# Sine and cosine ahead of the float32 head in SyncE's queue: a rotary embedding kernel on one core

## Chip, cores and metric

One core of a Trainium2 chip runs the whole kernel. The metric is the device time of one execution in microseconds (us). Engines are named as in the profile: DVE is VectorE, ACT is ScalarE, POOL is GpSimd, SP is SyncE; the core has 16 DMA engines, which the transfers of all queues share. The clock granted to TensorE was 1.00; the kernel has no matrix multiplication.

## The reference

```python
# x: (8, 2048, 16, 64), cos and sin: (2048, 32), all float32
x1 = x[..., :32]
x2 = x[..., 32:]
out1 = x1 * cos - x2 * sin      # cos and sin broadcast over batch and heads
out2 = x1 * sin + x2 * cos
out = concatenate([out1, out2], axis=-1)
```

Each of the 8 batches is 8.39 MB in and 8.39 MB out. Nothing is reused between batches but the two tables of 256 KB.

## The kernel before, in words

**Tiles.** A batch is one tile `xt` of 128 partitions by 16 rows of the sequence (J = 16) by 16 heads by 64, in float16. Five such tiles exist (NBUF = 5), so batch b + 5 takes the place of batch b. Loads (L52) and stores (L60) go through GpSimd's queue (q0 of the profile, "software_dynamic"), which converts from and to float32 on the way. A transfer of a whole tile is one instruction on POOL and 8 data packets on each of the 16 DMA engines.

**The opening.** The first two rows of batch 0 (JA = 2) don't come through GpSimd. SyncE loads them as float32 into the tile `head` (L36, 1 MB), then the tables `sin_f` (L44) and `cos_f` (L45), 256 KB each, through its own queue (q1, "hardware_dynamic"). ScalarE casts head into the first two rows of batch 0's tile (L84), makes `sin_h` of `sin_f` in two instructions (L88, and L89 with the sign turned) and `cos_h` of `cos_f` (L90). The remaining 14 rows of batch 0 come through GpSimd's queue as its first transfer.

**A rotation** is three VectorE instructions on a tile, or on some of its rows: `v` = swapped halves times sine (L73), `xt` times cosine in place (L79), plus `v` (L81). The first two rows of batch 0 are rotated first, by themselves, and the first of them is stored at once (L100); then the other 14 rows, then whole batches.

**The close.** The last batch goes out in three parts: rows 0 to 8 (L130) and 9 to 13 (L132) through GpSimd's queue, and the last two rows by a cast into `head` (L140) and SyncE (L141), which waits until the part of L130 has landed.

**What sets the order.** The program is handed to a planner, which orders each engine's instructions by their place in the program and by costs it estimates, and puts in the waits. The kernel adds a few edges that order GpSimd's queue without a wait ("NoSync"): the first row's store after load 1, load 2 after it, the rest of batch 0's store after it, the last part after the gate. By the trace GpSimd issued loads 0 and 1; the first row; loads 2, 3, 4; the stores of batch 0's rest and batch 1; loads 5 and 6; stores 2 and 3; load 7; stores 4, 5 and 6; the two parts of batch 7. POOL issues in that order, so an instruction that waits holds all behind it: loads 5, 6 and 7 each wait until the store of the batch whose tile they take has landed.

Of the kernel before, what the change touches and what calls it, by code (L numbers as in the profile page):

```python
# [1 line left out]

# [4 lines left out]


@with_exitstack  # L10
def kernel(
    ctx: ExitStack,
    tc: tile.TileContext,
    x: bass.AP,
    cos: bass.AP,
    sin: bass.AP,
    out: bass.AP,
):
    nc = tc.nc
    f16 = mybir.dt.float16  # L20
    f32 = mybir.dt.float32

    B, S, H, D = x.shape
    Dh = D // 2
    P = nc.NUM_PARTITIONS
    J = S // P
    NBUF = 5

    const_pool = ctx.enter_context(tc.tile_pool(name="rope_const", bufs=1))
    io_pool = ctx.enter_context(tc.tile_pool(name="rope_io", bufs=NBUF))  # L30
    tmp_pool = ctx.enter_context(tc.tile_pool(name="rope_tmp", bufs=1))

    JA = 2
    head = const_pool.tile([P, JA, H, D], f32)
    x0 = x[0].rearrange("(p j) h d -> p j (h d)", j=J)
    nc.sync.dma_start(  # L36
        out=head.rearrange("p j h d -> p (j h d)"),
        in_=x0[:, 0:JA, :].rearrange("p j f -> p (j f)"),
    )
    sin_f = const_pool.tile([P, J, Dh], f32)  # L40
    cos_f = const_pool.tile([P, J, Dh], f32)
    cos_h = const_pool.tile([P, J, Dh], f16)
    sin_h = const_pool.tile([P, J, D], f16)
    nc.sync.dma_start(out=sin_f, in_=sin.rearrange("(p j) d -> p j d", j=J))  # L44
    nc.sync.dma_start(out=cos_f, in_=cos.rearrange("(p j) d -> p j d", j=J))  # L45

    loads = []

    def load(b):
        xt = io_pool.tile([P, J, H, D], f16)  # L50
        j0 = JA if b == 0 else 0
        dma = nc.gpsimd.dma_start(  # L52
            out=xt[:, j0:J, :, :].rearrange("p j h d -> p (j h d)"),
            in_=x[b].rearrange("(p j) h d -> p j (h d)", j=J)[:, j0:J, :].rearrange("p j f -> p (j f)"),
        )
        loads.append(dma)
        return xt

    def store(b, xt, j0=0):
        return nc.gpsimd.dma_start(  # L60
            out=out[b].rearrange("(p j) h d -> p j (h d)", j=J)[:, j0:J, :].rearrange("p j f -> p (j f)"),
            in_=xt[:, j0:J, :, :].rearrange("p j h d -> p (j h d)"),
        )

    def rotate(xt, j0, j1):
        v = tmp_pool.tile([P, J, H, D], f16)
        n = j1 - j0
        js = slice(j0, j1)
        shape = [P, n, H, 2, Dh]
        sin_b = sin_h[:, js, :].rearrange("p j (e d) -> p j e d", e=2).unsqueeze(2).to_broadcast(shape)  # L70
        cos_b = cos_h[:, js, :].unsqueeze(2).to_broadcast([P, n, 2 * H, Dh])
        xe = xt[:, js, :, :].rearrange("p j h (e d) -> p j h e d", e=2)
        nc.vector.tensor_mul(  # L73
            out=v[:, js, :, :].rearrange("p j h (e d) -> p j h e d", e=2),
            in0=xe[:, :, :, ::-1, :],
            in1=sin_b,
        )
        xw = xt[:, js, :, :].rearrange("p j h (e d) -> p j (h e) d", d=Dh)
        nc.vector.tensor_mul(out=xw, in0=xw, in1=cos_b)  # L79
        xa = xt[:, js, :, :].rearrange("p j h d -> p (j h d)")  # L80
        nc.vector.tensor_add(out=xa, in0=xa, in1=v[:, js, :, :].rearrange("p j h d -> p (j h d)"))  # L81

    tiles = [load(b) for b in range(2)]
    nc.scalar.copy(  # L84
        out=tiles[0][:, 0:JA, :, :].rearrange("p j h d -> p (j h d)"),
        in_=head.rearrange("p j h d -> p (j h d)"),
    )
    nc.scalar.copy(out=sin_h[:, :, Dh:D], in_=sin_f)  # L88
    nc.scalar.mul(out=sin_h[:, :, 0:Dh], in_=sin_f, mul=-1.0)  # L89
    nc.scalar.copy(out=cos_h, in_=cos_f)  # L90
    rotate(tiles[0], 0, JA)
    def part(b, j0, j1):
        return (
            out[b].rearrange("(p j) h d -> p j (h d)", j=J)[:, j0:j1, :].rearrange("p j f -> p (j f)"),
            tiles[b][:, j0:j1, :, :].rearrange("p j h d -> p (j h d)"),
        )

    def store_rows(b, j0, j1):
        dst, src = part(b, j0, j1)
        return nc.gpsimd.dma_start(out=dst, in_=src)  # L100

    first = store_rows(0, 0, 1)
    tc.add_manual_dep(
        first.ins,
        loads[1].ins.name,
        mybir.DependencyInfo(mybir.DependencyClass.NoSync, mybir.DependencyReason.DATA),
        reason="order of the ring",
    )
    tiles += [load(b) for b in range(2, NBUF)]
    tc.add_manual_dep(  # L110
        loads[2].ins,
        first.ins.name,
        mybir.DependencyInfo(mybir.DependencyClass.NoSync, mybir.DependencyReason.DATA),
        reason="order of the ring",
    )
    for b in range(B):
        rotate(tiles[b], JA if b == 0 else 0, J)
        if b < B - 1:
            st = store(b, tiles[b], 1 if b == 0 else 0)
            if b == 0:  # L120
                tc.add_manual_dep(
                    st.ins,
                    first.ins.name,
                    mybir.DependencyInfo(mybir.DependencyClass.NoSync, mybir.DependencyReason.DATA),
                    reason="order of the ring",
                )
        if b + NBUF < B:
            tiles.append(load(b + NBUF))
    dst, src = part(B - 1, 0, 9)
    gate = nc.gpsimd.dma_start(out=dst, in_=src)  # L130
    dst, src = part(B - 1, 9, J - JA)
    rest = nc.gpsimd.dma_start(out=dst, in_=src)  # L132
    tc.add_manual_dep(
        rest.ins,
        gate.ins.name,
        mybir.DependencyInfo(mybir.DependencyClass.NoSync, mybir.DependencyReason.DATA),
        reason="order of the ring",
    )
    dst, src = part(B - 1, J - JA, J)
    nc.scalar.copy(out=head.rearrange("p j h d -> p (j h d)"), in_=src)  # L140
    end = nc.sync.dma_start(out=dst, in_=head.rearrange("p j h d -> p (j h d)"))  # L141
    tc.add_manual_dep(
        end.ins,
        gate.ins.name,
        mybir.DependencyInfo(mybir.DependencyClass.Sync, mybir.DependencyReason.DATA),
        reason="the last rows go out behind this part",
    )


# [1 line left out]
_INS = ['x', 'cos', 'sin']  # L151
_OUTS = [((8, 2048, 16, 64), 'float32')]


# [23 lines left out]
```

## Time and profile before

| What | Value |
|---|---|
| Median of 3 runs | 317.05 us (316.58 to 317.15) |
| The profiled execution: its time, its span | 316.67 us, 314.9 us |
| DVE, POOL, ACT busy | 209.1, 9.9, 6.8 us |
| Head: issued, landed after | 0.74, 4.8 us |
| Sine: issued, landed after | 1.16, 13.4 us |
| Cosine: issued, landed after | 1.63, 31.9 us |
| First rotation instruction; first row's store issued | 15.79; 36.95 us |
| Rotation of batch 0's rest begins | 36.69 us |
| Last rotation: begins, ends | 236.73, 262.9 us |
| SyncE's last transfer: issued, landed after | 305.64, 8.4 us |

The span runs from the first to the last instruction of the profiled execution. The page of the profile gives busy time by engine, then the span in 40 slices (each digit is a busy share in tenths; in the DMA row the mean of the 16 engines), the DMA queues, the chain of work that ended last, and the groups of instructions by line with the idle time ahead of them. Further views of the same trace used below are the waits, the instructions in order of time (start, duration, engine, line, operation, and in brackets the idle time before it and what ended that), the chain in order of time, and the records of the DMA packets (queue, size, start, duration).

### The profile page before, as it was taken

Reading aid. Unit: us, or ns where it says so; the run is one execution under the profiler, and the core shown is the slowest. Engines: PE = TensorE matmul, PEld = TensorE weight load, DVE = VectorE, ACT = ScalarE, POOL = GpSimd, SP = SyncE. Lnnn points to the kernel's source line nnn. Section 1 sums busy time; section 2 is a strip of 40 time slices with the busy share of each in tenths; the row PEclk is TensorE's granted clock in tenths of the full one; section 3 lists DMA queues with packets and bytes.
Section 4 is the critical chain, followed back from the end, with each engine's and each line's share of the span. In section 5 each row is a group of like instructions: output and inputs, shape, how many; then the busy total and the mean of one; then the engine's idle time right before and its main releaser. Section 6 shows DMA issues by size and latency. Waiting matters only on the chain.

```text
span 314.9 us, 122 instructions
## 1 busy us (share of the span) xinstructions
DVE 209.1 (66%) x27; ACT 6.8 (2%) x6; POOL 9.9 (3%) x22
## 2 busy tenths in 40 slices
DVE  0010699999999999999999999995009993000000
ACT  4100000000000000000000000000000002000000
POOL 1000200000000000010000000200000001000000
DMA  9899999999999899999999999999999999999997
GB/s 280 184 262 206 200 266 200 200 262 204 200 200 325 375 492 407 400 350 250 200 200 237 362 400 400 491 441 266 200 316 416 400 400 524 408 400 400 433 443 323
DMA packets 3168, 101.71 MB, mean 323 GB/s; under 512 B 352, under 2 KB 352, under 8 KB 736
## 3 DMA queue, kind: packets, MB, share of 16 engines
q0 software_dynamic: 2592, 99.09, 98.1%
q1 hardware_dynamic: 576, 2.62, 2.2%
HBM read 67.63 MB, written 67.11 MB: 428 GB/s over the span
## 4 chain that ended last, share of the span: by engine, by line
DVE 25%; DMA 22%; issue 18%; another core or an unknown queue 17%; ACT 1%; POOL 1%; SPq 0%; POOLq 0%; DVEq 0%; ACTq 0%
DMA xt<-in_x_dram 12%; DMA cos_f<-in_cos_dram 10%; DVE xt L81 8%; DVE xt L79 8%; DVE v L73 8%; ACT head L140 1%; POOL out_dram L60 0%; POOL xt L52 0%; ACT cos_h L90 0%; SPq L44 0%; SPq L36 0%; POOLq L52 0%; DVEq L73 0%; ACTq L140 0%
## 5 line engine op out<-in xcount | busy, mean ns | idle before, releaser
L73 DVE TENSOR_TENSOR v<-xt,sin_h 128x16384 f16<-128x16384 f16 (+2 forms) x9 | 69.7, 7744 | 36.0 <-DMA xt<-in_x_dram 20.0
L79 DVE TENSOR_TENSOR xt<-xt,cos_h 128x16384 f16<-128x16384 f16 (+2 forms) x9 | 69.7, 7744 | 17.4 <-ACT cos_h L90 17.2
L81 DVE TENSOR_TENSOR xt<-xt,v 128x16384 f16<-128x16384 f16 (+2 forms) x9 | 69.7, 7745 | 0.3
L52 POOL DMA_DIRECT2D xt<-in_x_dram x8 | 4.4, 556 | 110.4 <-DMA out_dram<-xt 109.6
L140 ACT CAST head<-xt 128x2048 f32<-128x2048 f16 x1 | 1.9, 1897 | 228.8 <-DVE xt L81 228.8
L60 POOL DMA_DIRECT2D out_dram<-xt x7 | 3.7, 535 | 63.6 <-DVE xt L81 63.6
L84 ACT CAST xt<-head 128x2048 f16<-128x2048 f32 x1 | 1.9, 1897 | 3.5 <-DMA head<-in_x_dram 3.5
L130 POOL DMA_DIRECT2D out_dram<-xt x1 | 0.5, 531 | 45.6 <-DVE xt L81 45.6
L100 POOL DMA_DIRECT2D out_dram<-xt x1 | 0.5, 536 | 34.5 <-DVE xt L81 34.5
L84 ACT ACT_TABLE_LOAD x1 | 1.3, 1283 | 0.7 <-PEq L162 0.7
L90 ACT CAST cos_h<-cos_f 128x512 f16<-128x512 f32 x1 | 0.6, 617 | 17.8 <-DMA cos_f<-in_cos_dram 17.8
L88 ACT CAST sin_h<-sin_f 128x512 f16<-128x512 f32 x1 | 0.6, 617 | 7.2 <-DMA sin_f<-in_sin_dram 7.2
L89 ACT ACTIVATE sin_h<-sin_f 128x512 f16<-128x512 f32 x1 | 0.6, 624 | 0.0
L132 POOL DMA_DIRECT2D out_dram<-xt x1 | 0.5, 531 | 0.0
L162 POOL MEMSET const-float32-0.0<- 128x1 f32 x1 | 0.1, 98 | 0.2 <-issue 0.2
L162 POOL MEMSET const-bfloat16-1.0<- 128x1 bf16 x1 | 0.1, 101 | 0.0
L162 POOL MEMSET const-float32-1.0<- 128x1 f32 x1 | 0.1, 98 | 0.0
L162 POOL MEMSET const-uint8-127<- 128x1 uint8 x1 | 0.1, 98 | 0.0
## 6 DMA issues: line engine op xcount, KB each, us to landing
xt<-in_x_dram POOLq DMA_DIRECT2D x7, 4096.0 KB, 38.3
out_dram<-xt POOLq DMA_DIRECT2D x1, 7680.0 KB, 60.9
out_dram<-xt POOLq DMA_DIRECT2D x1, 4608.0 KB, 42.4
xt<-in_x_dram POOLq DMA_DIRECT2D x1, 3584.0 KB, 22.3
out_dram<-xt POOLq DMA_DIRECT2D x1, 2560.0 KB, 47.9
head<-in_x_dram SPq DMA_DIRECT2D x1, 1024.0 KB, 4.8
out_dram<-head SPq DMA_DIRECT2D x1, 1024.0 KB, 8.4
out_dram<-xt POOLq DMA_DIRECT2D x1, 512.0 KB, 7.8
```

The costliest lines, as they stand in the source:

```text
L52: dma = nc.gpsimd.dma_start(out=xt[:, j0:J, :, :].rearrange("p j h d -> p (j h d)"), in_=x[b].rearrange("(p j) h d -> p j (h d)", j=J)[:, ...
L60: return nc.gpsimd.dma_start(out=out[b].rearrange("(p j) h d -> p j (h d)", j=J)[:, j0:J, :].rearrange("p j f -> p (j f)"), in_=xt[:, j0:J ...
L73: nc.vector.tensor_mul(out=v[:, js, :, :].rearrange("p j h (e d) -> p j h e d", e=2), in0=xe[:, :, :, ::-1, :], in1=sin_b,)
L79: nc.vector.tensor_mul(out=xw, in0=xw, in1=cos_b)
L81: nc.vector.tensor_add(out=xa, in0=xa, in1=v[:, js, :, :].rearrange("p j h d -> p (j h d)"))
L84: nc.scalar.copy(out=tiles[0][:, 0:JA, :, :].rearrange("p j h d -> p (j h d)"), in_=head.rearrange("p j h d -> p (j h d)"),)
L88: nc.scalar.copy(out=sin_h[:, :, Dh:D], in_=sin_f)
L89: nc.scalar.mul(out=sin_h[:, :, 0:Dh], in_=sin_f, mul=-1.0)
L90: nc.scalar.copy(out=cos_h, in_=cos_f)
L100: return nc.gpsimd.dma_start(out=dst, in_=src)
L130: gate = nc.gpsimd.dma_start(out=dst, in_=src)
L140: nc.scalar.copy(out=head.rearrange("p j h d -> p (j h d)"), in_=src)
```

## The change

SyncE's three opening DMAs are issued in the order sine, cosine, head instead of head, sine, cosine. Besides, the program is written in another form: a table `plan` lists the loads (L), rotations (R) and stores (S) with batch and rows, a loop runs it, and every transfer of GpSimd's queue has a NoSync edge to the one before it, where before a few had. The cast of head into batch 0's tile now stands in the program ahead of that tile's load by GpSimd; it stood behind the loads of batches 0 and 1. The sizes of the transfers, the tiles and their number, the arithmetic and the close are the same. The kind "L4" occurs in no row of the plan.

```diff
     head = const_pool.tile([P, JA, H, D], f32)
-    x0 = x[0].rearrange("(p j) h d -> p j (h d)", j=J)
-    nc.sync.dma_start(
-        out=head.rearrange("p j h d -> p (j h d)"),
-        in_=x0[:, 0:JA, :].rearrange("p j f -> p (j f)"),
-    )
...
     nc.sync.dma_start(out=sin_f, in_=sin.rearrange("(p j) d -> p j d", j=J))
     nc.sync.dma_start(out=cos_f, in_=cos.rearrange("(p j) d -> p j d", j=J))
+    x0 = x[0].rearrange("(p j) h d -> p j (h d)", j=J)
+    nc.sync.dma_start(
+        out=head.rearrange("p j h d -> p (j h d)"),
+        in_=x0[:, 0:JA, :].rearrange("p j f -> p (j f)"),
+    )
...
+    plan = (
+        ("L", 0, 2, 16), ("L", 1, 0, 16), ("R", 0, 0, 2), ("S", 0, 0, 1),
+        ("L", 2, 0, 16), ("L", 3, 0, 16), ("L", 4, 0, 16),
+        ("R", 0, 2, 16), ("S", 0, 1, 16), ("R", 1, 0, 16), ("S", 1, 0, 16),
+        ("L", 5, 0, 16), ("L", 6, 0, 16),
+        ("R", 2, 0, 16), ("S", 2, 0, 16), ("R", 3, 0, 16), ("S", 3, 0, 16),
+        ("L", 7, 0, 16),
+        ("R", 4, 0, 16), ("S", 4, 0, 16), ("R", 5, 0, 16), ("S", 5, 0, 16),
+        ("R", 6, 0, 16), ("S", 6, 0, 16), ("R", 7, 0, 16),
+    )
...
+    def ring(out, in_, **kw):
+        nonlocal last
+        dma = nc.gpsimd.dma_start(out=out, in_=in_, **kw)
+        if last is not None:
+            behind(dma, last, mybir.DependencyClass.NoSync)
+        last = dma
+        return dma
...
-    tiles = [load(b) for b in range(2)]
-    nc.scalar.copy(
-        out=tiles[0][:, 0:JA, :, :].rearrange("p j h d -> p (j h d)"),
-        in_=head.rearrange("p j h d -> p (j h d)"),
-    )
+    flat = head.rearrange("p j h d -> p (j h d)")
+    tiles[0] = io_pool.tile([P, J, H, D], f16, name="xt")
+    nc.scalar.copy(out=held(0, 0, JA), in_=flat)
     nc.scalar.copy(out=sin_h[:, :, Dh:D], in_=sin_f)
     nc.scalar.mul(out=sin_h[:, :, 0:Dh], in_=sin_f, mul=-1.0)
     nc.scalar.copy(out=cos_h, in_=cos_f)
...
+    for what, b, j0, j1 in plan:
+        if what == "L":
+            if b not in tiles:
+                tiles[b] = io_pool.tile([P, J, H, D], f16, name="xt")
+            ring(held(b, j0, j1), rows(x, b, j0, j1))
...
+        elif what == "S":
+            ring(rows(out, b, j0, j1), held(b, j0, j1))
+        else:
+            rotate(b, j0, j1)
```

## The prediction, as put on record

> **What bounds the kernel now.** I read the busy line by engine first, then the DMA lines of the page, then the waits, then the chain, and last the stretch around the change in order of time.
>
> ```profile
> span 314.9 us, 122 instructions
> ...
> DVE 209.1 (66%) x27; ACT 6.8 (2%) x6; POOL 9.9 (3%) x22
> ...
> DMA  9899999999999899999999999999999999999997
> ...
> q0 software_dynamic: 2592, 99.09, 98.1%
> q1 hardware_dynamic: 576, 2.62, 2.2%
> HBM read 67.63 MB, written 67.11 MB: 428 GB/s over the span
> ```
>
> No compute engine is near its span, but the sixteen DMA engines are busy in every slice: q0 (GpSimd's queue) 98.1% and q1 (SyncE's) 2.2% make 100%. Busy could still mean slow, so I check the pace with the waits of GpSimd's queue.
>
> ```profile
> 120.75 8.69 DVE L79 TENSOR_TENSOR xt<-xt,cos_h 128x16384 f16<-128x16384 f16 x1
> 121.38 0.53 POOL L52 DMA_DIRECT2D xt<-in_x_dram x1 [34.74 <-DMA out_dram<-xt]
> ...
> 140.66 0.53 POOL L52 DMA_DIRECT2D xt<-in_x_dram x1 [18.75 <-DMA out_dram<-xt]
> ...
> 198.37 0.53 POOL L52 DMA_DIRECT2D xt<-in_x_dram x1 [56.12 <-DMA out_dram<-xt]
> ...
> 236.73 8.69 DVE L73 TENSOR_TENSOR v<-xt,sin_h 128x16384 f16<-128x16384 f16 x1 [20.02 <-DMA xt<-in_x_dram]
> ```
>
> Each of these starts as a transfer lands: the rest of batch 0's store, batch 1's store, batch 2's store (behind the loads of 5 and 6), and the load of batch 7 (behind batch 3's store). Between them lie 1, 3 and 2 whole batches of 8.39 MB: 140.66 - 121.38 = 19.28, (198.37 - 140.66) / 3 = 19.24, (236.73 - 198.37) / 2 = 19.18 us. That is one steady 435 GB/s. The whole traffic at it, (67.63 + 67.11) MB / 435 GB/s, is 309.7 us of a 314.9 us span. So the queue is never empty, and the order and volume of its transfers set the end. The last DVE instruction ends at 262.9 us, 52 us ahead of it.
>
> The chain of waits tells another story at the start, and it is the change's story:
>
> ```profile
> 1.63 31.86 DMA cos_f<-in_cos_dram
> 33.49 0.02 issue
> 33.52 0.63 ACT cos_h L90
> 34.14 0.02 issue
> 34.17 1.24 DVE xt L79
> ```
>
> Cosine, 256 KB, takes 31.86 us and holds VectorE back. The trace's packet records say why (worked out per queue and size; times in us):
>
> ```
> queue   bytes  what            packets  start of first..last  one takes
> SyncE    8192  head            128       1.73 ..  4.86        0.309 (each engine's first 0.37 to 1.04)
> SyncE    2048  sine, cosine    256       4.72 .. 30.62        0.084 alone, 0.096 beside GpSimd's
> GpSimd  28672  batch 0 load    128       5.12 .. 20.99        2.129
> GpSimd  32768  batch loads 1-7 896      22.75 .. 233.91       2.431
> ```
>
> Each engine gets 8 data packets of every transfer and one small one for the semaphore. Up to 5.12 us it serves SyncE's alone; from 5.12 to 5.62, engine by engine, GpSimd's begin, and then one SyncE packet passes per GpSimd packet. Sine lands at 14.6, cosine at 33.5: nine turns of 2.1 to 2.4 us apart.
>
> **The change part by part.** *The plan of the GpSimd queue.* Its rows are, one by one, the order in which the trace shows GpSimd issuing: loads 0 and 1, one row of batch 0, loads 2 to 4, stores 0 and 1, loads 5 and 6, stores 2 and 3, load 7, stores 4 to 6, two parts of store 7. Same transfers, same instructions (22 on POOL), nothing added: 0 us. No added edge between two of them makes an engine wait for another.
>
> *SyncE's order.* SyncE issues at 0.74, 1.16 and 1.63 now and will again, with sine, cosine, head in the slots. Sine's first packet comes at about 1.73 (head's now does). Sine and cosine together take 16 x 0.084 = 1.34 us per engine; the cold first packets cost head now 4.72 - 1.73 - 8 x 0.309 = 0.5 us, which I take over. So head starts at 1.73 + 0.5 + 1.34 = 3.6 and by 5.4, when GpSimd's packets come, 1.8 / 0.309, some 5 to 6 of its 8 packets are through. Three or four are left with the semaphore's, each behind 2.13 us: head lands near 5.4 + 4 x 2.4 = 15, instead of 5.5. Bounds: 8, if only one is left; 5.6 + 9 x 2.44 = 27.6, if none has passed.
>
> *The path behind it.* ScalarE's cast of head takes 1.90, the two casts of sine (starts 14.61 and 15.13) 1.14 if they stay behind it, then VectorE's three instructions at 1.24: the first row of batch 0 is ready near 15 + 1.9 + 1.1 + 3.7 = 22 instead of 36.7 (34.3 by the late bound). The rest of batch 0 can start when its load has landed, at 1.25 + 22.3 = 23.6, instead of 36.69: VectorE is **13 us earlier**. The store of batch 0's rest is issued near 47 instead of 59.92, that of batch 1 near 73 instead of 86.11.
>
> *Where the 13 us go.* The stores join a queue that is full: loads 2 to 4 stand ahead of them. The rest of batch 0's store still lands at 120.8, so load 5 still waits for its buffer until 121.4: POOL's wait there grows from 34.74 to about 48. Rotations 2, 3 and 4 follow at 26.2 each (3 x 8.73) and end near 151.5; rotation 5 then waits for load 5, rotation 6 ends near 212, and rotation 7 waits for load 7, which lands at 236.7 as before. VectorE's 20.02 us there become about 25. Nothing after 236.7 moves. What is late next is the queue itself. Gain on the path: 0.
>
> *What is left is the work of the DMA engines.* The bytes are the same. In the window before GpSimd's packets there is enough from SyncE either way: sine, cosine and head last until 1.73 + 0.5 + 1.34 + 2.47 = 6.0, past 5.62, so no engine idles. Some twelve sine and cosine packets now served at 0.096 will be served at 0.084: -0.15. The cold start is not seen for 2048-byte packets: at best its 0.5 us vanishes (-0.65 in all); at worst each of the two later transfers pays another 0.5 (+1.0). I take about 0, since the cold cost is that of the first packet on an engine, and there is one in either order.
>
> The records price the small packets: 2048 bytes in 0.084 us are 24.4 GB/s per engine, head's 8192 in 0.309 are 26.5, and one SyncE packet passes per GpSimd packet. [...]
>
> **Sum.** The profiled execution took 316.67: the span of 314.9 and 1.77 around it. 316.67 + 0 = 316.7, with -0.65 to +1.0 as bounds. It lies 0.38 below the median of the runs, 317.05, so for the median I say **317.0**. About 0.2% (0.6 us) is what a measurement of this kernel can tell from no change.
>
> **Rivals.** *The early start reaches the end.* If the loads and stores could follow the rotations, 13 us would come off: 304. For it: the chain starts with cosine. Against it: 435 GB/s without a gap, and 20 us of waiting ahead of rotation 7. 2%.
>
> *A quicker start of the engines.* The cold cost nearly vanishes with small packets: 317.05 - 0.7 = 316.3. For it: it is the only slack in the stream. [...] 6%.
>
> *A slower start.* Cosine and head each pay their own cold start: 317.05 + 1.0 = 318.0. For it: three small starts in a row; against: sine's first packets behind head took at most 0.148. 5%.
>
> *Batch 0's load waits for ScalarE (slower).* In the new text the cast of head into batch 0's tile stands ahead of that tile's load. If the dependency were kept by tile and not by rows, POOL's first DMA would wait for it, and with it everything in POOL's queue. Head would then land alone at 6.5, the cast end at 8.4, the load be issued at 8.5 and, as now (5.12 - 1.25 = 3.9 later), move its first packet at 12.4. The engines would stand idle from 6.0: +6.4, **323.4**. It costs as soon as the load is issued after 6.0 - 3.9 = 2.1. Against it: now the load stands first, and the cast starts at 5.54, eighteen us before that load lands, into the same tile. 5%.
>
> *The change doesn't do what it says:* three loads with no dependency could still be ordered head first by the planner. Then 317.05. 3%.
>
> Head that comes very late is no rival of its own: POOL runs dry only if the first row's store is issued after load 1 has landed (23.6 + 8 x 2.43 = 43.0), and the late bound gives 34.3.
>
> **How the numbers follow.** The forecast has 79% (own range 316.5 to 317.6) and the planner's rival 3%: 82% within 0.2%. Faster: 6 + 2 = 8%. Slower: 5 + 5 = 10%. The range, 316.2 to 318.2, takes in the bounds of the cold start on the median and leaves out the 2% and the 5% far off.
>
> **What would show it.** Right: sine and cosine landed before 6 us, head near 15; batch 0's rest rotating near 24; the load of batch 5 still issued near 121.4, that of batch 7 near 198.4; a longer wait ahead of rotation 7; DMA slices all at 9. Wrong: a POOL wait ahead of batch 0's load, a low digit in the first DMA slice, a pace other than 19.2 us per batch, or a load of batch 7 that lands at another time than 236.7, with the difference in it.

## The result, and the profile after

The changed kernel takes 318.22 us in the median of 22 runs (316.39 to 319.39), the kernel before 316.94 (316.58 to 317.42, 22 runs): a ratio of 1.0034, 95% interval 1.0020 to 1.0049. It is slower by a third of a per cent, and its runs lie 3.0 us apart where those of before lie 0.8: nine of the 22 take 317.4 us or less, as before, the others up to 319.39. The forecast of no change was wrong; 318.22 lies just above the upper end of its range (318.2), and so near to it by chance, since the mechanism is one that none of its cases has.

The page of the changed kernel, the same lines as before:

```profile
span 317.6 us, 121 instructions
...
DVE 209.1 (66%) x27; ACT 6.7 (2%) x6; POOL 9.9 (3%) x22
...
DMA  8999999999999899999999999999999999999995
...
q0 software_dynamic: 2592, 99.09, 97.5%
q1 hardware_dynamic: 576, 2.62, 2.2%
HBM read 67.63 MB, written 67.11 MB: 424 GB/s over the span
```

The first slice of the DMA row is an 8 where a 9 stood, q0's share fell from 98.1% to 97.5%, and the span grew by 2.7. The profiled execution took 319.38 us, nearly the longest of the 22, so it shows the full loss; no trace of a shorter one exists. The bytes, packets and POOL instructions are the same. The instructions in order of time show where the 2.7 us came in:

```profile
0.74 0.38 SPq L39 DMA_DIRECT2D sin_f<-in_sin_dram  x1
1.17 0.43 SPq L40 DMA_DIRECT2D cos_f<-in_cos_dram  x1
...
1.64 0.42 SPq L42 DMA_DIRECT2D head<-in_x_dram  x1
3.61 0.62 ACT L123 CAST sin_h<-sin_f 128x512 f16<-128x512 f32 x1 [1.59 <-DMA sin_f<-in_sin_dram]
...
27.88 1.90 ACT L122 CAST xt<-head 128x2048 f16<-128x2048 f32 x1 [22.61 <-DMA head<-in_x_dram]
...
33.58 7.63 DVE L110 TENSOR_TENSOR v<-xt,sin_h 128x14336 f16<-128x14336 f16 x1
...
124.02 0.53 POOL L95 DMA_DIRECT2D xt<-in_x_dram  x1 [40.48 <-DMA out_dram<-xt]
...
143.32 0.53 POOL L95 DMA_DIRECT2D xt<-in_x_dram  x1 [18.76 <-DMA out_dram<-xt]
...
162.12 8.69 DVE L110 TENSOR_TENSOR v<-xt,sin_h 128x16384 f16<-128x16384 f16 x1 [0.87 <-DMA xt<-in_x_dram]
...
201.00 0.53 POOL L95 DMA_DIRECT2D xt<-in_x_dram  x1 [56.10 <-DMA out_dram<-xt]
...
239.39 8.69 DVE L110 TENSOR_TENSOR v<-xt,sin_h 128x16384 f16<-128x16384 f16 x1 [24.94 <-DMA xt<-in_x_dram]
```

The four events that were at 121.38, 140.66, 198.37 and 236.73 are at 124.02, 143.32, 201.00 and 239.39: later by 2.64, 2.66, 2.63 and 2.66. The pace between them is the old one, (201.00 - 143.32) / 3 = 19.23 us per batch. So nothing was lost between 124 and 239 us, and all of it before. VectorE meanwhile began the rest of batch 0 at 33.58 in place of 36.69 and waits 24.94 in place of 20.02 ahead of the last rotation: its lead is waited away, as the prediction has it.

The packet and semaphore records of the two traces show the loss itself. The 16 DMA engines post their semaphore steps one by one as their share of a transfer is done (352 landings for 22 transfers, 16 each); "first" and "last" are the earliest and the latest engine (us, worked out from the records). The records carry no engine's number: what is said here and below of single engines is worked out from the starts, ends and landings.

```
                                   before            after
SyncE packets per engine ahead
  of GpSimd's first                13 to 18          18 (sine, cosine)
GpSimd's first packets start       5.12 .. 5.62      3.35 .. about 5.7
engines at work, of 16, in
  3.5-4.0  4.0-4.5  4.5-5.0        16   16   16      11.5  11.8  12.6
  5.0-5.5  5.5-6.0  6.0-6.5        16   16   16      14.4  15.4  15.5
head's first packet                1.73              5.6
landing of       load 0            23.02 .. 23.55    23.39 .. 26.45
  first, last    rest of store 0   120.27 .. 120.79  121.03 .. 123.44
                 load 7            236.14 .. 236.64  236.90 .. 239.29
                 SyncE's last      313.52 .. 314.04  314.27 .. 316.74
```

Sine and cosine are through the engines by 3.4 to 3.8, and then more than a quarter of the engines (4.5 of 16) stand still, the last of them for some 2 us. Twelve engines have their first GpSimd packet by 4.09, four between 4.84 and 5.66. Every transfer is cut into 16 equal shares (each engine gets 8 data packets of it and one small one), and the engines that started some 2 us behind did not catch up: the distance between the first and the last engine is 3.1 us at load 0 and still 2.4 to 2.5 at the end of the kernel, where twelve engines post between 314.27 and 314.70 and four between 315.72 and 316.74.

Standing still is not all of it. On average an engine ended 1.2 us later (the mean of the 16 last steps is 313.71 before, 314.93 after). Of this, idle time after 3.5 us makes 0.5 ((4.5 + 4.2 + 3.4 + 1.6 + 0.6 + 0.5) x 0.5 / 16). Most of the rest is packets that took longer: GpSimd's first two on an engine took 2.33 and 2.42 us in the mean, where both took 2.13 before. Why they did is not shown. The time is that of the last engine, 2.7 us later.

### The profile page after: what moved, and what is told of

It is laid out like the page before. It is cut to its first block, busy times and chain, and to the rows that moved or that the text cites. A ratio compares the mean times of both kernels' runs of the same rounds, so it can differ in the third digit from the quotient of the medians.

```text
span 317.6 us, 121 instructions
## 1 busy us (share of the span) xinstructions
DVE 209.1 (66%) x27; ACT 6.7 (2%) x6; POOL 9.9 (3%) x22
## 3 DMA queue, kind: packets, MB, share of 16 engines
q0 software_dynamic: 2592, 99.09, 97.5%
## 4 chain that ended last, share of the span: by engine, by line
DVE 44%; DMA 20%; issue 18%; ACT 1%; POOL 0%; SPq 0%; DVEq 0%; ACTq 0%; POOLq 0%
DVE v L110 16%; DVE xt L118 14%; DVE xt L116 14%; DMA xt<-in_x_dram 12%; DMA head<-in_x_dram 8%; ACT xt L122 1%; ACT head L140 1%; POOL out_dram L95 0%; SPq L40 0%; SPq L39 0%; DVEq L110 0%; ACTq L140 0%; POOLq L95 0%
```

## The experiments

The leading theory was the hole: in the new order the DMA engines run out of work between SyncE's and GpSimd's packets, unequally, and the latest engine sets the end. The rivals: the new form of the program costs the time; tables in front cost it by themselves; head comes late, by its size, its place, or for another reason; GpSimd's start is uneven by itself. Kernels of one group ran on one chip beside the kernel before; ratios are to it, with 95% intervals, and differ slightly from the quotient of the medians. In the code below, (head) stands for head's load and `...` for what is left out of a line.

### The form alone, and the order alone

`e1_form_only` is the new form with SyncE's old order; `e2_order_only` is the old form with SyncE's new order.

```diff
 # e1, against the changed kernel
+    (head)
     nc.sync.dma_start(out=sin_f, ...)
     nc.sync.dma_start(out=cos_f, ...)
-    (head)
 # e2, against the kernel before: the same lines the other way round
```

> The plan's form with SyncE's old order (head, sine, cosine). Gap theory (after sine and cosine the DMA engines have nothing to do for up to 2 us, unequally, and the latest one stays behind to the end): head is 64 KB per engine and covers that time, so GpSimd's first packets start within 0.6 us of each other, a landing's 16 semaphore steps stay within 0.6 us, and the time is that of before, 316.9 (ratio 0.999 to 1.001). Form theory (the cast ahead of the load in the program, or the edges, cost the time): 318.2, as the change.

> The old form with SyncE's order sine, cosine, head. Gap theory: 318.2 in the median, runs scattered from 316.4 to 319.4 as the latest engine's start falls, landings spread over 2 us or more. Form theory: 316.9, landings within 0.6 us.

Measured: e1 317.17 us, 0.9995 (0.9986 to 1.0004); e2 319.36 us (316.86 to 326.07), 1.0048 (1.0029 to 1.0068). The form is free, and the order alone is the whole effect. In the profiled execution of e1 (317.7 us, its longest) GpSimd's first packets start within 0.7 us of each other, but the landings of load 0 are 1.2 us apart and later ones 1.3, where 0.6 was expected: three of the first packets took 2.57 to 2.74 us and not 2.13. In that of e2 (319.39 us) they start from 3.46 to 5.75 and the landings stay 2.65 us apart to the end. One of e2's twelve executions took 326.07; the ratio leaves it out, no trace of it exists, and it stays unexplained.

### Two of the three in front

`e3_sin_head_cos` puts head second; `e4_tables_from_act` and `e8_head_from_act` use ScalarE's queue beside SyncE's.

```diff
 # e3, against the changed kernel, as e4 and e8
     nc.sync.dma_start(out=sin_f, ...)
-    nc.sync.dma_start(out=cos_f, ...)
     (head)
+    nc.sync.dma_start(out=cos_f, ...)
 # e4
-    nc.sync.dma_start(out=sin_f, ...)
-    nc.sync.dma_start(out=cos_f, ...)
+    nc.scalar.dma_start(out=sin_f, ...)
+    nc.scalar.dma_start(out=cos_f, ...)
 # e8
-    nc.sync.dma_start(out=head..., ...)
+    nc.scalar.dma_start(out=head..., ...)
```

> The plan's form with SyncE's order sine, head, cosine. Gap theory: sine's 16 KB and head's 64 KB per engine follow each other without a hole until about 1.73 + 0.5 + 0.67 + 2.47 = 5.4, so GpSimd's packets are covered and the time is 316.9, landings within 0.6 us; head lands near 5.8 and cosine, now the third, near 25. Rival (head is late because of its size or of the order, not because it stands third): head's first packet comes near 5.6 again, the hole opens already at 2.7 and the time is 318.2 or more.

> The plan's form, head issued by SyncE and both tables at the same time by ScalarE's queue. Gap theory: three transfers share the engines from 1.7 to about 6.0 without a hole, the time is 316.9 and landings stay within 0.6 us, although all three land before 8 and VectorE's rotation of batch 0's rest starts near 24 instead of 36.7. A theory by which the early rotation is worth something would have 304 to 316; one by which any early small transfer in front costs a cold start would have 318.

> The change with head issued by ScalarE's queue at the same time as the tables by SyncE's: tables in front as in the change, but the engines are fed until about 6.0. Gap theory: no hole, landings within 1 us, 316.4 to 317, although VectorE starts the rest of batch 0 near 24, 10 us ahead of the change. Rival (tables in front cost time by themselves): 318 to 319.5.

Measured: e3 316.62 us, 0.9981 (0.9972 to 0.9989); e4 316.78 us, 0.9982 (0.9973 to 0.9990); e8 316.82 us, 0.9987 (0.9978 to 0.9995). In all three the loss is gone, and 0.1 to 0.2% more. GpSimd's first packets start at 5.2 to 5.8, nearly all engines are at work from 2.5 us on and all from 3.0, and the landings at the end are 0.98, 0.35 and 0.60 us apart. So in e3 and e8 (0.9981, 0.9987) a small table in front cost nothing, with head's 8192-byte packets ahead of GpSimd's first as well. One expectation missed: cosine did not land early in e4 and e8. As the second of its queue it came behind GpSimd's first packets and landed at 26.13 and 23.99, so the rest of batch 0 began at 29.33 and 27.18, not at 24.

### No head, a short head, a small third transfer

`e5_no_head` drops head: all 16 rows of batch 0 come through GpSimd. `e7_short_head` has the old order with one row in head. `e6_third_small` puts a fourth, useless transfer of 98 KB between cosine and head.

```diff
 # e5, against the changed kernel
-    nc.sync.dma_start(out=head..., in_=x0[:, 0:JA, :]...)
-    nc.scalar.copy(out=held(0, 0, JA), in_=flat)
-        ("L", 0, 2, 16),
+        ("L", 0, 0, 16),
 # e6, against the changed kernel
+    again = const_pool.tile([P, 6, Dh], f32)
...
     nc.sync.dma_start(out=cos_f, ...)
+    nc.sync.dma_start(out=again, in_=sin.rearrange("(p j) d -> p j d", j=J)[:, 0:6, :])
 # e7, against e1: head[:, 0:1] and row 0 alone; the plan loads and rotates rows 1 to 15
-        ("L", 0, 2, 16),  ("R", 0, 0, 2),  ("R", 0, 2, 16),
+        ("L", 0, 1, 16),  ("R", 0, 0, 1),  ("R", 0, 1, 16),
```

> SyncE loads the two tables alone; all 16 rows of batch 0 come through GpSimd's queue, the same bytes in all. Gap theory (the hole is GpSimd's own uneven start once SyncE's packets are gone): its first packets again start anywhere from 3.4 to 5.9, landings spread over 2 us or more, the time is 318 to 319.5. Rival (head's late packets hold up some engines): without head the first packets start within 0.6 us of each other and the time is 316.5 to 317.

> The change with a small third transfer (six rows of sine again, 768 bytes per partition, into a tile that nobody reads) between cosine and head; head is the fourth. It adds 98 KB, 0.2 us of the engines. If the third place is what is late, the small transfer's first packet comes only near 5.6, behind GpSimd's first, and the hole stays: 318 to 319.5. If head was late for its size, the small transfer follows cosine by 3.7 without a hole of its own, and head's packets come near 5.6 behind it.

> The plan's form, SyncE's old order, but head has one row in place of two (512 KB; the other 15 rows of batch 0 come through GpSimd, the same bytes in all). Gap theory: SyncE's first two transfers last until 1.73 + 0.5 + 8 x 0.16 + 0.67 = 4.2 in place of 5.4, so about half the hole opens: landings spread over 1 to 2 us, 317.5 to 318.5. Rival (only which transfer stands first or last counts, not how long the engines are fed): 316.9 to 317.2, as with two rows.

Measured: e5 318.61 us (316.46 to 319.39), 1.0032 (1.0013 to 1.0051): the loss and the scatter of the change without any head at all. Fifteen engines get their first GpSimd packet at 3.42 to 3.83, one at 5.67, and that one keeps the landings 3.0 us apart. Head's late packets are not the cause.

e7 317.03 us (316.99 to 317.59), 0.9994 (0.9985 to 1.0002): my estimate missed. Half the cover cost nothing: SyncE's first two transfers end at 4.5 to 5.4, GpSimd's first packets start at 4.16 to 5.08, no engine stands still until 6.5. Here the hole did not grow in step with the time for which SyncE feeds the engines. All of head and sine, 18 packets on each engine, and none of cosine went ahead of GpSimd's first. It also shows that 5.12 us, which the prediction took for the time when GpSimd's packets come, is only when the lot of SyncE's packets ahead of them is done ("lot" here: the packets of SyncE that an engine runs ahead of GpSimd's first).

e6 327.39 us (four runs, 326.48 to 329.04), 1.0335 (1.0309 to 1.0361), far over both theories. Its engines happened to start evenly in the profiled execution, the shortest of the four (GpSimd's first packets at 3.40 to 3.70), and what costs is another thing, in the order of time:

```profile
43.71 1.90 ACT L124 CAST xt<-head 128x2048 f16<-128x2048 f32 x1 [38.57 <-DMA head<-in_x_dram]
...
49.68 0.54 POOL L97 DMA_DIRECT2D out_dram<-xt  x1 [47.23 <-DVE xt L120]
50.21 1.59 POOL L97 DMA_DIRECT2D xt<-in_x_dram  x3
...
131.18 0.53 POOL L97 DMA_DIRECT2D xt<-in_x_dram  x1 [31.80 <-DMA out_dram<-xt]
```

98 KB are 0.2 us of the engines' time at 435 GB/s (0.4 us by the records of these packets), but they are 9 more packets on each engine, and beside GpSimd's each waits for a turn: head lands at 43.7 instead of 27.9, 15.8 / 9 = 1.8 us for each. The first row's store is issued at 49.68, behind the landing of load 1 (43.52), so GpSimd's queue, which holds loads 2 to 4 behind that store, was empty until its next packets at 50.79: 7.3 of the 9 us that this execution (326.48) lies above the kernel before (317.33). This is the limit that the prediction put at 43 us, met by accident. The small transfer's first packet came at 5.57, behind GpSimd's first: size is not what made a third transfer late.

### Later work from GpSimd, and head as the second of two queues

`e9_pool_later` is the change with a memset of 2.66 us ahead of GpSimd's first load; `e11_pool_later_old_order` is the same with SyncE's old order; `e10_cos_from_act` is the change with cosine issued by ScalarE.

```diff
 # e9 and e11 (e11 also has head, sine, cosine)
     tiles[0] = io_pool.tile([P, J, H, D], f16, name="xt")
+    nc.gpsimd.memset(held(0, JA, JA + 3), 0.0)
 # e10, against the changed kernel
-    nc.sync.dma_start(out=cos_f, ...)
+    nc.scalar.dma_start(out=cos_f, ...)
```

> The change, with GpSimd kept busy by one memset of three rows of batch 0's tile ahead of its first load, some 2 to 4 us, so that its packets come later. If head, the third transfer, is ready by itself and only loses its turn to GpSimd's first packets, it now follows cosine at about 3.7 and feeds the engines until about 6.0: the hole closes although GpSimd is later, all three land before 7, landings within 1 us, 316.4 to 317.5. If head is late by itself (first packet near 5.6 whatever GpSimd does), every engine stands still from 3.7 to 5.6 and the time is 318.5 to 320.

> The change with cosine issued by ScalarE's queue, so that head is the second transfer of SyncE's and the third of all. If a queue's third transfer is what is late, head now follows sine and cosine without a hole: 316.4 to 317, landings within 1 us, head landed before 8.5. If the engines take some 13 to 18 packets each before GpSimd's turn comes, whichever queue they are from, head is left behind GpSimd's first packets again: 318 to 319.5, head landed near 25.

> The plan's form with SyncE's old order and the same memset ahead of GpSimd's first load. SyncE's three transfers feed the engines until about 6.0, so a load that is issued 2 to 4 us later should cost at most about 1 us, and less than 0.5 if its packets come by 6.5: 316.5 to 318. It prices the memset for the kernel above.

Measured: e9 319.14 us, 1.0065 (1.0053 to 1.0077); e11 317.03 us, 0.9997 (0.9988 to 1.0006); e10 316.56 us (316.39 to 316.81), 0.9981 (0.9972 to 0.9990).

e11 and e9 differ in SyncE's order alone. A load issued 2.5 us later (3.70 for 1.25) cost nothing behind head, sine and cosine: all three follow one another almost without a hole until 6.4, and GpSimd's packets take over at 5.88 to 6.42. So in e11, where the engines were at work, the third transfer was not late. Behind sine and cosine the engines run dry twice, at 3.5 (8.4 of 16 at work) and again at 6.0 to 7.5 (11.9 to 13.8 at work): head's first packets come from 3.42 on, not all at once and not all at 5.6, and GpSimd's from 6.19 to beyond 7.9, where e11's were there by 6.42. All six runs of e9 pay (319.03 to 319.37). Neither of the two stories that I had written for e9 is right as it stands: some of the engines that had run dry got their next work late, from either queue.

e10 has the same three transfers early, with head behind sine on SyncE's queue while cosine is on ScalarE's. No engine stands still after 3.0 us, GpSimd's first packets start at 5.37 to 5.69, and the landings stay 0.26 us apart to the end, the least of all. Neither expectation had this: 5 to 6 of head's 8 packets went ahead of GpSimd's first and the rest did not, so head landed neither before 8.5 nor near 25. Its beginning in order of time:

```profile
0.74 0.39 ACTq L40 DMA_DIRECT2D cos_f<-in_cos_dram  x1
0.74 0.38 SPq L39 DMA_DIRECT2D sin_f<-in_sin_dram  x1
...
1.17 0.42 SPq L42 DMA_DIRECT2D head<-in_x_dram  x1
...
15.32 1.90 ACT L122 CAST xt<-head 128x2048 f16<-128x2048 f32 x1 [9.28 <-DMA head<-in_x_dram]
...
23.84 7.63 DVE L110 TENSOR_TENSOR v<-xt,sin_h 128x14336 f16<-128x14336 f16 x1 [2.85 <-DMA xt<-in_x_dram]
```

Both tables land by 4.6, head at 15.3, and VectorE starts the rest of batch 0 at 23.84 when its load has landed: the very course that the prediction drew for the change. It is worth 0.2% against the kernel before, and that is not VectorE's 13 us: e3, which starts VectorE 5.6 us later (29.45), has the same ratio. The evenness of the engines fits it, but no run shows that it is all. By its interval e10 beats both kernels.

### GpSimd's start by itself

`e12_gpsimd_alone` and `e13_gpsimd_first` hold SyncE's head back behind VectorE, so that GpSimd's queue would start on unused engines. Each ran once.

```diff
 # against the changed kernel; hf is head's tile, one row per partition
+    nc.vector.memset(hf, 0.0)
+    for _ in range(4):
+        nc.vector.tensor_add(out=hf, in0=hf, in1=hf)
     (head, sine, cosine)
+    # e13 alone: NoSync edges from sine and cosine to head
```

> The plan's form, SyncE's old order, but its first DMA waits behind a memset and four additions of VectorE on head's tile (some 8 us or more), so GpSimd's queue starts on engines that nobody else has used. Read for the start alone: head, sine and cosine then take 27 turns beside GpSimd's packets, the first row's store comes after load 1 has landed, and the whole is tens of us longer (340 to 370). If GpSimd's first packets reach the engines unevenly by themselves, their starts are spread over 2 us again (3.4 to 5.7). If only engines that ran dry behind SyncE's packets start late, all 16 start within 0.6 us of each other, near 3.4.

> The plan's form with SyncE's order head, sine, cosine held by edges, and SyncE's first DMA behind a memset and four additions of VectorE on head's tile (11.0 us in the run before), so GpSimd's queue starts on engines that SyncE has not used. Read for the start alone; head, sine and cosine then need 27 turns beside GpSimd's packets, and the queue runs empty behind load 1: 335 to 370. If GpSimd's first packets reach the engines unevenly by themselves, their starts are spread over 1 to 2.3 us again (3.4 to 5.7). If only engines that ran dry behind SyncE's packets start late, all 16 start within 0.6 us of each other, near 3.4.

e12 did not do what it was meant to do: the planner put sine and cosine ahead of the waiting head. Read for what it is, it is the change with head issued at 12.34 us: 320.63 us (317.07 for the kernel before beside it), 14 engines with their first GpSimd packet at 3.35 to 3.78, one at 4.43 and one at 5.5 or later, load 0 landing from 21.87 to 24.78. Like e5 it has the hole with no head about. Here the distance shrank, to 1.6 us: the first row's store was issued at 42.90, when the engines in front had just finished load 1 (42.75) and the last had not (45.50), so those in front had to wait.

e13 did: 326.39 us (317.38 beside it; 335 to 370 was expected), most of it because the first row's store came at 49.19, behind load 1, as in e6. On engines that SyncE had not touched, all 16 first packets of GpSimd start between 2.61 and 3.02, within 0.41 us, 1.4 to 1.8 after the issue at 1.25. These packets took unequal times, 2.5 to 3.3 us, and the landings of load 0 lie 1.2 us apart. So in e13 GpSimd's queue by itself did not start unevenly, and its packets were there before the time at which sine and cosine are done in the change, 3.4 to 3.8. The late start was seen only on engines that had just emptied a lot of SyncE's packets.

### All of them side by side

For each profiled execution but those of e6, e12 and e13, which lose more elsewhere, from the records: what an engine does ahead of GpSimd's first packet, how far apart the engines are at the last landing, and the time.

```
                       ahead of GpSimd's first        first GpSimd packets   engines apart   time of this
                       packet on an engine            start (us)             at the end      execution
e10                    sine, cosine, part of head     5.37 .. 5.69           0.26            316.39
e4                     sine, head                     5.22 .. 5.75           0.35            316.55
before                 head, part of sine             5.12 .. 5.62           0.52            316.67
e8                     sine, head                     5.42 .. 5.62           0.60            317.21
e11 (GpSimd later)     head, sine, cosine             5.88 .. 6.42           0.63            316.92
e7 (head of 1 row)     head, sine                     4.16 .. 5.08           0.73            317.11
e3                     sine, head                     5.17 .. 5.79           0.98            317.30
e1                     head, part of sine             5.12 .. 5.78           1.32            317.70
e9 (GpSimd later)      sine, cosine, part of head     6.19 .. past 7.9       1.97            319.37
after                  sine, cosine                   3.35 .. about 5.7      2.47            319.38
e2                     sine, cosine                   3.46 .. 5.75           2.65            319.39
e5 (no head)           sine, cosine                   3.42 .. 5.67           2.97            319.24
```

By and large the time follows the distance between the engines: from 0.26 us and 316.39 to about 2.5 and 319.4. It does not follow the start of VectorE (36.5 us in e1, 23.8 in e10 and 33.6 in the change).

## Why the prediction was wrong, point by point

**What bounds the kernel: right.** The queue of the DMA engines sets the end, at 19.2 us per batch in both kernels, and a wait ahead of the last rotation takes back whatever VectorE gains: 24.94 us, where 25 was forecast. VectorE's lead was 3.1 us and not 13, but rotation 5 did wait for load 5, as forecast (by 0.87 us at 162.12, and by 7.66 in e10), and from there on the transfers alone set that wait: it is 24.96 in e10.

**The plan costs nothing: right** (e1, 0.9995). So the rival of a load that waits for ScalarE's cast is out: GpSimd's first issue is at 1.25 us in both.

**Head lands near 15, VectorE 13 us earlier: wrong in size.** Head landed at 27.85, a shade past the late bound of 27.6: hardly any of its packets went ahead of GpSimd's. VectorE was 3.1 us earlier. Between 9.9 and 24.5 head's packets passed in turns some 2.45 us apart, one (0.32) to one of GpSimd's (2.13). As forecast, nothing hung on it.

**The step that failed** is the sentence that sine, cosine and head "last until 1.73 + 0.5 + 1.34 + 2.47 = 6.0, past 5.62, so no engine idles". Its addition takes for granted that an engine goes from cosine straight on to head, and so it put the idle time at nothing. The runs showed that where SyncE alone feeds the engines first and GpSimd issues at 1.25, an engine runs some 13 to 18 of SyncE's packets ahead of GpSimd's first, of 8192, 4096 (e7) or 2048 bytes: before, these were head and part of sine and lasted until 5.1 to 5.6; after, they were the 18 of sine and cosine, 2048 bytes at 0.084 us, gone by 3.4 to 3.8. Then some engines stand still for up to 2 us, though head has been issued at 1.64 and GpSimd's packets were ready by 3.0 in e13. Whether 18 packets or two transfers are the limit, no run can tell: in all of these at most a packet or two of SyncE's third transfer went ahead.

**The other rivals.** SyncE did issue sine first, so the change does what it says. Neither the slower nor the quicker start in the cold was it, in the form that they had: sine and cosine were done by 3.4 to 3.8, where 1.73 + 0.5 + 1.34 = 3.6 was forecast; the first packet on an engine, now of 2048 bytes, took 0.28 to 0.60 us, against 0.084 for those behind it. But "there is one in either order" missed that GpSimd's first two packets took 0.2 and 0.3 us longer in the new order.

**A second slip was behind the failed step:** it took 5.12 us, from the trace of before, for a time that belongs to GpSimd's queue. It belonged to what ran ahead; e7 moved it to 4.16, the change to 3.35, e13 to 2.61. The 3.9 us in the price of the load that waits (+6.4) is the same time, and so too long: e13 has 1.4 to 1.8.

**And the stake was set too low.** The bound of +1.0 us was worked out from cold starts that every engine pays alike. The loss is unequal, 1.2 us on average (0.5 of it idle) and 2.7 on the last engine, and the last counts. That the runs of the change are so far apart (316.39 to 319.39) would be the same thing: an execution whose engines all change over at once would be as fast as e10, while one with a single late engine pays some 2.5 us (e5, 319.24). e6's profiled execution shows that an even start can come behind sine and cosine; no trace of a fast execution of the change exists, so this is argued. The sign that would have shown the sum wrong was named (a low digit in the first DMA slice, load 7 late with the whole difference in it), and it was there.

**What stays open:** why an engine that has emptied its lot of SyncE's packets gets the next work up to 2 us late, and why only some engines do, and why GpSimd's first packets then take longer. No run shows a mechanism. The counts alone are shown: 13 to 18 packets of SyncE's ahead of GpSimd's first (before; 18 in the change and in e7), and behind it one SyncE packet to one of GpSimd's.

## What to carry to other kernels

Where DMA bounds a kernel, don't count its bytes alone: ask whether all 16 engines have work from the first packet to the last. In the change the engines that started some 2 us late were still 2.4 to 2.5 us behind at the end, and every landing waited for them; in e12, where the engines in front had to wait for a store, the distance shrank, to 1.6 us. In this kernel it cost nothing to have a transfer of 0.5 or 1 MB among the first two of SyncE's queue (0.9994 in e7, 0.9981 in e3), with one table of 256 KB ahead of it in e3; in e10 (0.9981) both tables were early, one of them through a second queue. And where a time in the trace (5.12 us here) is taken into a forecast, ask first what it belongs to: the queue that starts then, or the work that ended.

## What the runs showed of the hardware that was not expected

- GpSimd's first packets started 1.4 to 1.8 us after the issue on unused engines (e13), SyncE's 1.0 to 1.3 (sine in the change, 0.74 to 1.74 and later). Behind SyncE's packets GpSimd's came 2.1 to 4.5 us after an issue at 1.25 (the change, e3), by what ran ahead.
- The first packet of GpSimd's queue took longer on an engine that had no work: 2.5 to 3.3 us in e13 for 28672 bytes, and 2.5 to 3.1 on the four late engines of the change, against 2.13 in the median of that size (before and the change).
- A DMA of 98 KB, 0.2 us at 435 GB/s, cost 10 us (e6): beside a full queue its 9 packets per engine put 16 us on the landing of the transfer behind it, and that was enough to starve another queue.
